# Fourteen half-product pairs instead of twelve in the up projection of a fused decoder layer, with one term kept in DRAM

## The chip, the cores and the metric

The kernel runs on one core of a Trainium2 chip. The metric is the device time of one launch in microseconds; the median of several runs is compared. The engines are PE (matrix products, with PEld for its weight loads), DVE, ACT and POOL (elementwise work), and SP, which here only issues DMA transfers; ACT and POOL issue some transfers too.

## The reference

One decoder layer in float32 for 512 tokens of 1024 channels: two token mixers side by side (an RWKV-7 recurrence and a sparse attention), their merge, and then a gated feed-forward part with a causal convolution of width 3 between its up projection and the gate. The change lies in the feed-forward part, which is, cut to what matters:

```python
h = rms_norm(x, g)                       # 512 x 1024
u = h @ w_up                             # 1024 -> 2 * 2816 (gate and value)
u = causal_conv_width_3(u) + bias        # per channel, along the tokens
gate, value = split(u)
y = silu(gate) * value                   # 512 x 2816
out = x + rms_norm(y @ w_down, g2)       # 2816 -> 1024
```

## The kernel before

Float32 products are made from two parts: each operand is split into a high and a low part, and three products (high by high, high by low, low by high) are added up in PSUM. ACT copies the high part of a weight chunk (128x512), and DVE or POOL subtracts it from the raw chunk to get the low part. In tile names `r` is the raw chunk, `h` its high and `l` its low part: `sw166r`, `sw166h`, `sw166l`.

**Up stage.** The 5632 columns of `w_up` are 44 blocks of 128: pair j (0 to 21) has block 2j, which gives the gate, and block 2j+1, which gives the value. An *ordinary pair* multiplies its two blocks by all 512 tokens, with 24 matmuls of 512 columns for each block (`mm3`, L232 to L234). A *half-product pair* (`seven(j)`) computes the 2x2 block product of weight halves and token halves by seven products instead of eight: 84 matmuls of 256 columns (L1567), five additions on DVE (L1572) and one copy on ACT (L1578). Of its seven weight chunks, four are sums of weight blocks. These are formed earlier in DRAM by DMAs with addition that POOL issues (`group_sums`, L251, eight for a group of two pairs). The token side's four sums and differences (`tf0` to `tf3`) are built on DVE and ACT in the early pairs (`token_forms`, L1498 to L1508).

Which pairs are half-product pairs stands in `SEVEN`; before, these are pairs 10 to 21. Their chunks come through a ring of buffers (`form_w`, with `sw` as name), five chunks ahead (`ahead`, `coming`): SP loads, ACT makes the high part (L134), POOL or DVE the low part (L172).

After a pair's products, ACT starts the convolution of each block (L1619), DVE does two more steps of it (`scalar_tensor_tensor`, STT in the text, L1620 and L1621), ACT applies the silu, and DVE or POOL multiplies gate and value (L1630, L1635). ACT stores the high part of the product in `ah` (L1638), DVE the low part in `al` (L1639).

**Down stage.** It also uses a seven-product form, with the 22 pairs in two halves of 11 (`KH`): for j < 11 the kernel keeps `y[rgt] - y[lft]` in place of `y[rgt]` (L1637); for j >= 11 it makes `t24`, which needs this difference of pair j−11 again, in DVE steps L1647 to L1649, and stores it to DRAM (`t24d`). Before, the difference is put together again from `ah` and `al`. The stage then runs seven products over eleven weight chunks each (`down`, L1745 to L1747, six matmuls for a chunk, `dw0r` and so on for the chunks); `down_w` loads and splits a chunk. Sums of down weights are formed in DRAM too (`down_sums`, L272, 48 DMAs). All of these weight-sum DMAs are one chain, `ws`, of which `next(ws)` issues the next; each call stands at a fixed place in the program.

Within an engine the order is a scheduler's: it follows the program, subject to when buffers of the pools come free. Where the program says `keep_in_program_order` or `behind`, that sets it.

Of the kernel before, what the change touches and what calls it, by code (L numbers as in the profile page):

```python
# [10 lines left out]
F32 = mybir.dt.float32  # L11
# [16 lines left out]
RAWB = 4  # L28
SEVEN = (10, 11, 12, 13, 14, 15, 16, 17, 18, 19, 20, 21)
SGRP = 2  # L30
# [22 lines left out]
def hybrid_layer(ctx: ExitStack, tc: tile.TileContext, a, out, dbg=None, stop=None):  # L53
# [200 lines left out]
    def weight_sums():  # L254
        gs = [group_sums(x, f) for x, f in zip(SGROUPS, fsum)]
        for i in range(0, len(gs), 4):
            for _ in range(8):
                for y in gs[i:i + 4]:
                    next(y)
                    yield  # L260

    t24d = dr.tile([KH, 128, S], F32, name="t24d", bufs=1)
    dsum = [[dr.tile([k.stop - k.start, 128, 512], F32, name=f"ds{i}{k.start}", bufs=1) for i in range(4)] for k in DCH]
# [1215 lines left out]
    with pool("ff") as ff:  # L1479
# [66 lines left out]
        def form_seq():  # L1546
            for j in SEVEN:
                n = SEVEN.index(j)
                fs = [f[n % SGRP] for f in fsum[n // SGRP]]
                for x, eng in (((0, 0), po), (2, po), (1, ve), (3, po), ((0, 1), po), (4, po), ((1, 1), ve)):  # L1550
                    src = fs[x - 1] if isinstance(x, int) else a["up4"][x[0], x[1], UPOS[j]]
                    ahead.append(form_w(src, f"sw{j}{x if isinstance(x, int) else 5 + 2 * x[0] + x[1]}", eng))
                    yield
# [4 lines left out]
        def seven(j):  # L1558
# [30 lines left out]
            return g, v  # L1589

        side = token_forms()
        sctx2 = ExitStack()
        for j in range(22):
# [4 lines left out]
            if j == SEVEN[0]:  # L1598
                for _ in side:
                    pass  # L1600
            if j in SEVEN:
                sv_ = seven(j)
            for x in range(2):
# [19 lines left out]
                if j < SEVEN[0]:  # L1623
                    for _ in range(1):
                        next(side, None)
                if (j > 2 or x == 0 if j < SEVEN[0] else x == 0 and j < 19):
                    next(ws, None)
# [8 lines left out]
            if j < KH:  # L1636
                ve.tensor_tensor(y[:, rgt], y[:, rgt], y[:, lft], op=OP.subtract)  # L1637
            sc.activation(ah[:, j, :], y, AF.Copy)  # L1638
            ve.tensor_tensor(al[:, j, :], y, ah[:, j, :].bitcast(F32), op=OP.subtract)  # L1639
            if j >= KH:  # L1640
                if j == KH:
                    t2ctx = ExitStack()
                    t2 = pool("t2", "left", t2ctx)
                else:
                    sy.dma_start(t24d[j - 1 - KH], t24)
                t24 = t2.tile([128, S], F32, tag="t24", name=f"t24{j}", bufs=2)
                ve.tensor_tensor(t24[:, lft], y[:, rgt], ah[:, j - KH, rgt].bitcast(F32), op=OP.subtract)  # L1647
                ve.tensor_tensor(t24[:, lft], t24[:, lft], al[:, j - KH, rgt].bitcast(F32), op=OP.subtract)
                ve.tensor_tensor(t24[:, rgt], y[:, lft], t24[:, lft], op=OP.subtract)  # L1649
# [5 lines left out]
        def down_w(f, k):  # L1655
# [6 lines left out]
            if n < 8 or n > 9 and n % 8 < 2 or n % 8 >= 6:  # L1662
                raw = wp.tile([128, 512], F32, tag="raw", name=f"dw{n}r", bufs=RAWB)
            elif n < 10:
                raw = t2.tile([128, 512], F32, tag="draw", name=f"dw{n}r", bufs=2)
            else:
                raw = ep.tile([128, 512], F32, tag="draw", name=f"dw{n}r", bufs=4)
            load, high = sy.dma_start(raw, src), sc.activation(hi, raw, AF.Copy)
            low = (po if n % 3 == 1 else ve).tensor_tensor(lo, raw, hi.bitcast(F32), op=OP.subtract)
            if n >= 10:  # L1670
                keep(load)
# [8 lines left out]
        with pool("ep") as ep:  # L1680
            res2 = ep.tile([128, 4, 512], F32, name="res2")
            pa, u4 = ([ep.tile([128, 512], F32, name=f"{n}{i}") for i in range(2)] for n in ("pa", "uf"))
            t24 = ep.tile([128, KH, S], F32, name="t24")
            g3 = ep.tile([128, D], F32, name="gb4")
            s2, x2 = {}, {}

# [62 lines left out]
            def down(m, f, r, n, bank, side=iter(()), at=7):  # L1749
                p = [bank(f"dn{m}{i}") for i in range(2)]  # L1750
                for k in range(KH - TL if m == 6 else KH):
# [3 lines left out]
                    if k in TURN[m]:  # L1755
                        next(turned)
                    if k % 3 == 0:
                        next(ws, None)
# [160 lines left out]
```

## Time and profile before

| what | us |
|---|---|
| median of 3 runs | 1135.24 |
| fastest and slowest run | 1135.18, 1135.8 |
| the profiled execution, its own time | 1133.54 |
| its span | 1131.5 |

The profiled execution is a single one and 1.70 us under the median of the runs. The span is the time from the first to the last instruction on the engines.

### The profile page before, as it was taken

Reading aid. Unit: us, or ns where it says so; the run is one execution under the profiler, and the core shown is the slowest. Engines: PE = TensorE matmul, PEld = TensorE weight load, DVE = VectorE, ACT = ScalarE, POOL = GpSimd, SP = SyncE. Lnnn points to the kernel's source line nnn. Section 1 sums busy time; section 2 is a strip of 40 time slices with the busy share of each in tenths; the row PEclk is TensorE's granted clock in tenths of the full one; section 3 lists DMA queues with packets and bytes.
Section 4 is the critical chain, followed back from the end, with each engine's and each line's share of the span. In section 5 each row is a group of like instructions: output and inputs, shape, how many; then the busy total and the mean of one; then the engine's idle time right before and its main releaser. Section 6 shows DMA issues by size and latency. Waiting matters only on the chain.

```text
span 1131.5 us, 21237 instructions
## 1 busy us (share of the span) xinstructions
PE 1110.3 (98%) x7704; PEld 909.6 (80%) x7704; DVE 750.4 (66%) x1432; ACT 639.2 (56%) x1258; POOL 613.5 (54%) x615
## 2 busy tenths in 40 slices
PE   9999999999999999999999999999999999999997
PEld 7888888877888887766666777888888899998885
DVE  4236664735666552597787754755785699997986
ACT  6447763554666434386675654543554576665554
POOL 4346674535666453566545543540578777753431
PEclk9999999999999999999999999999999999999999
DMA  7524468632666896516576465777568678968783
GB/s 256 144 81 124 141 166 217 182 104 86 182 146 172 235 242 216 132 48 194 171 218 181 127 149 166 231 240 220 136 185 202 207 263 227 266 181 302 228 283 113
DMA packets 117002, 208.33 MB, mean 184 GB/s; under 512 B 37025, under 2 KB 39905, under 8 KB 110754
## 3 DMA queue, kind: packets, MB, share of 16 engines
q1 hardware_dynamic: 93538, 144.05, 40.6%
q0 software_dynamic: 7504, 48.50, 18.4%
q10 hardware_dynamic: 15856, 14.42, 4.0%
q8 instruction: 61, 1.00, 0.4%
q14 instruction: 43, 0.35, 0.1%
HBM read 179.60 MB, written 72.35 MB: 223 GB/s over the span
## 4 chain that ended last, share of the span: by engine, by line
PE 87%; DVE 5%; DMA 3%; POOL 2%; issue 1%; ACT 1%; SPq 0%; DVEq 0%; POOLq 0%; ACTq 0%
PE st L1567 4%; PE sg L1567 3%; PE dn L1745 3%; PE dn L1746 3%; PE dn L1747 3%; PE gt L348 3%; PE o L1218 3%; PE gt L349 3%; PE gt L350 3%; PE pt L150 3%; PE ub L1276 3%; PE pu L234 2%; PE ub L1278 2%; PE pu L232 2%; PE pu L233 2%; PE ub L1277 2%
## 5 line engine op out<-in xcount | busy, mean ns | idle before, releaser
L1166 ACT ACTIVATE p<-p,stt 128x384 f32<-128x384 f32 (+3 forms) x128 | 70.6, 554 | 33.4 <-DVE stt L1164 30.8
L1164 DVE CUSTOM_DVE_ANT_0 p<-s,rh 128x384 f32<-128x384 f32 (+3 forms) x128 | 59.2, 484 | 21.5 <-PE s L1150 17.9
L1138 POOL TENSOR_SCALAR p<-p,stt 128x512 f32<-128x512 f32 (+1 forms) x64 | 39.3, 622 | 38.7 <-DVE stt L1131 24.5
L1746 PE MATMUL dn<-hl,ah 128*128 128x512 f32 x148 | 57.6, 389 | 0.0
L1747 PE MATMUL dn<-hh,al 128*128 128x512 f32 x148 | 57.6, 389 | 0.0
L1745 PE MATMUL dn<-hh,ah 128*128 128x512 f32 x148 | 57.2, 389 | 0.0
L150 PE MATMUL pt<-ident,p 128*128 128x128 f32 x320 | 44.3, 273 | 1.2 <-DVE p L1140 1.2
L1157 PE MATMUL s<-kst,qs 128*128 128x512 f32 (+1 forms) x128 | 38.8, 394 | 5.8 <-DVE stt L1164 5.6
L150 PEld LDWEIGHTS pt<-ident,p 128*128 128x128 f32 x320 | 37.8, 141 | 6.9 <-DVE p L1140 1.6
L1218 PE MATMUL o<-PT,vt 128*64 128x384 f32 (+3 forms) x256 | 41.0, 443 | 0.0
L1209 ACT ACTIVATE PT<-pt 128x512 f32<-128x512 f32 x48 | 27.5, 587 | 10.4 <-PE pt L150 10.3
L1157 PEld LDWEIGHTS s<-kst,qs 128*128 128x128 f32 x128 | 21.2, 189 | 15.0 <-DVE stt L1164 11.8
L1140 DVE TENSOR_SCALAR p<-p,stt 128x512 f32<-128x512 f32 (+1 forms) x64 | 32.3, 532 | 0.7
L1747 PEld LDWEIGHTS dn<-hh,al 128*128 128x128 f32 x148 | 27.8, 188 | 5.8
L1745 PEld LDWEIGHTS dn<-hh,ah 128*128 128x128 f32 x148 | 27.8, 188 | 5.8
L1746 PEld LDWEIGHTS dn<-hl,ah 128*128 128x128 f32 x148 | 27.8, 188 | 5.7
L1218 PEld LDWEIGHTS o<-PT,vt 128*64 128x64 f32 x256 | 16.3, 136 | 18.3 <-issue 16.0
L272 POOL DMA_DIRECT2D ds<-in_down_dram x36 | 25.6, 710 | 7.3 <-DMA ds<-ds 7.3
L1620 DVE SCALAR_TENSOR_TENSOR u<-pu,cvec,u 128x511 f32<-128x511 f32 x20 | 15.0, 748 | 19.2 <-ACT u L1619 19.2
L1211 DVE COPY PT<-pt 128x512 f32<-128x512 f32 x32 | 21.8, 680 | 8.6 <-PE pt L150 8.5
L251 POOL DMA_DIRECT2D fs<-in_up_dram x36 | 26.0, 731 | 0.5 <-issue 0.4
L868 ACT ACTIVATE UV<-xs 64x256 f32<-64x256 f32 x16 | 6.0, 378 | 35.7 <-PE xs L861 35.3
(2206 smaller groups left out, 4242.4 us busy)
## 6 DMA issues: line engine op xcount, KB each, us to landing
fs<-in_up_dram POOLq DMA_DIRECT2D x36, 512.0 KB, 6.5
ds<-in_down_dram POOLq DMA_DIRECT2D x30, 512.0 KB, 6.1
fs<-fs POOLq DMA_DIRECT2D x12, 512.0 KB, 4.4
ds<-ds POOLq DMA_DIRECT2D x10, 512.0 KB, 5.7
gtd<-gt ACTq DMA_DIRECT2D x16, 256.0 KB, 4.8
qs<-qd SPq DMA_DIRECT2D x32, 128.0 KB, 3.6
g<-gtd SPq DMA_DIRECT2D x16, 256.0 KB, 3.6
t24d<-t SPq DMA_DIRECT2D x10, 256.0 KB, 5.4
```

The lines of the kernel that those rows point to most:

```text
L150: return te.transpose(o, i, ident)
L348: te.matmul(p, wh(k), hh[:, k, :], start=k == 0, stop=False)
L349: te.matmul(p, wh(k), hl[:, k, :], start=False, stop=False)
L1138: po.tensor_scalar(o.pe[e, b, k], o.pe[e, b, k], w, 1.0, op0=OP.mult, op1=OP.mult)
L1157: m = te.matmul(s_[:, :n], qt, kt[:, x, b, :n], start=x == 0, stop=x == 1)
L1164: ve.tensor_tensor_reduce(sb, parts[b], rh[e][:, (3 - qb) * 128:], -1.0, BIG, OP.add, OP.min, st[e][:, 0, i:i + 1])
L1166: sc.activation(sb, sb, AF.Exp, scale=-1.0, bias=st[e][:, 0, i:i + 1], accum_out=st[e][:, 1, i:i + 1])
L1218: te.matmul(acc[e * 64:e * 64 + 64, j * 128:], vt[:, j, b * 256 + g * 64:b * 256 + g * 64 + 64], m[e][:, c:c + n], start=False, stop=k == ...
L1567: te.matmul(p, w[y][:, ks], x[z][:, k, :], start=first and k + n == 0, stop=last and k == hf - 1 and n == 2, skip_group_check=True)
L1745: te.matmul(p, xh, w[0], start=first, stop=False)
L1746: te.matmul(p, xh, w[1], start=False, stop=False)
L1747: te.matmul(p, xl, w[0], start=False, stop=last)
```

## The change

Pairs 6 to 12, 14 to 16 and 18 to 21 are half-product pairs, fourteen of them. Pairs 13 and 17 lie between and are ordinary; a new function `plain(j)` runs them from the same ring of chunks, in the half layout. The weights in DRAM lie in the order of `SEVEN`, and the up weights' sums make seven groups of eight DMAs, where there were six. The pace of `next(ws)` is another: from pair 6 on one for each half-product pair and two for pairs 13 and 17, and in the down stage only from the third product on (`m > 1`).

For j < 11 ACT's queue stores `y[rgt] - y[lft]` in float32 to a DRAM tile `t1d`; for j >= 11 SP loads it back, two ahead, and `t24` takes it, so that one of its three DVE steps (L1648) is gone. At the down stage's start the copies of chunks 3 to 9 are put behind ACT's high copy of pair 20, chunks 8 and 9 use the ring's raw buffers, and a junk tile `p2jk` is allocated early.

```diff
-SEVEN = (10, 11, 12, 13, 14, 15, 16, 17, 18, 19, 20, 21)
+SEVEN = (6, 7, 8, 9, 10, 11, 12, 14, 15, 16, 18, 19, 20, 21)
...
+    t1d = dr.tile([KH, 128, 256], F32, name="t1d", bufs=1)
...
         def form_seq():
-            for j in SEVEN:
+            for j in range(SEVEN[0], 22):
+                if j not in SEVEN:
+                    for b, c, eng in ((0, 0, po), (0, 1, ve), (1, 0, po), (1, 1, ve)):
+                        ahead.append(form_w(a["up4"][b, c, UPOS[j]], f"sw{j}{b}{c}", eng))
+                        yield
+                    continue
...
+        def plain(j):
+            g, v = (pj if j % 2 else px)(f"sg{j}"), (pj if j % 2 else py)(f"sv{j}")
+            for p in (g, v):
+                for i in range(2):
+                    w = ahead.pop(0)
+                    for k in range(hf):
+                        ks = slice(k * 128, k * 128 + 128)
+                        for n, (y, z) in enumerate(((0, h2h), (0, h2l), (1, h2h))):
+                            te.matmul(p, w[y][:, ks], z[:, i * hf + k, :], start=i + k + n == 0,
+                                      stop=i == 1 and k == hf - 1 and n == 2)
+                    next(coming, None)
+            return g, v
+
+        def t1_load(k):
+            t = t2.tile([128, 256], F32, tag="t1", name=f"t1{k}", bufs=2)
+            sy.dma_start(t, t1d[k])
+            return t
...
-            if j in SEVEN:
-                sv_ = seven(j)
+            if j >= SEVEN[0]:
+                sv_ = (seven if j in SEVEN else plain)(j)
...
-                if (j > 2 or x == 0 if j < SEVEN[0] else x == 0 and j < 19):
+                if (j > 2 or x == 0 if j < SEVEN[0] else x == 0 or j not in SEVEN):
                     next(ws, None)
...
-            sc.activation(ah[:, j, :], y, AF.Copy)
+            high = sc.activation(ah[:, j, :], y, AF.Copy)
+            if j == 20:
+                last[high.ins.engine] = high
+            if j < KH:
+                tc.keep_in_program_order(sc.dma_start(t1d[j], y[:, rgt]))
...
+                    t1s = [t1_load(0), t1_load(1)]
...
-                ve.tensor_tensor(t24[:, lft], y[:, rgt], ah[:, j - KH, rgt].bitcast(F32), op=OP.subtract)
-                ve.tensor_tensor(t24[:, lft], t24[:, lft], al[:, j - KH, rgt].bitcast(F32), op=OP.subtract)
+                ve.tensor_tensor(t24[:, lft], y[:, rgt], t1s[j - KH], op=OP.subtract)
+                if j < 20:
+                    t1s.append(t1_load(j - KH + 2))
...
             elif n < 10:
-                raw = t2.tile([128, 512], F32, tag="draw", name=f"dw{n}r", bufs=2)
+                raw = sw.tile([128, 512], F32, tag="sraw", name=f"dw{n}r", bufs=4)
...
+            if WB <= n < 10:
+                behind(high)
...
+            ep.tile([128, 512], F32, tag="p2jk", name="p2jk", bufs=1)
...
-                    if k % 3 == 0:
+                    if m > 1 and k % 3 == 0:
                         next(ws, None)
```

The order on the engines moves at three places that the prediction speaks of. The first is ACT at the entry into the first half-product pair: before it is pair 10, with blocks 18 and 19 of the ordinary pair ahead of it (`pu18`, `pu19` in PSUM, `u18`, `u19` after the convolution; `ah` takes the high part of a pair's product).

```order
L1638 ACTIVATE ah_9042<-u17_9840 128x512
L134 ACTIVATE sw102h_9935<-sw102r_9937 128x512
L1619 ACTIVATE u18_9887<-pu18_9862,cvec_8504 128x512
L134 ACTIVATE sw101h_9941<-sw101r_9943 128x512
L134 ACTIVATE sw103h_9947<-sw103r_9949 128x512
L134 ACTIVATE sw104h_9987<-sw104r_9989 128x512
L134 ACTIVATE sw106h_9953<-sw106r_9955 128x512
L134 ACTIVATE sw108h_10005<-sw108r_10007 128x512
L1629 ACTIVATE u18_9887<-u18_9887 128x512
L134 ACTIVATE sw115h_10025<-sw115r_10027 128x512
L1619 ACTIVATE u19_9959<-pu19_9904,cvec_8504 128x512
```

After the change it is pair 6, with blocks 10 and 11 ahead of it.

```order
L1662 ACTIVATE ah_9047<-u9_9489 128x512
L1666 DMA t1d_142<-u9_9489 128x256
L1643 ACTIVATE u10_9540<-pu10_9515,cvec_8509 128x512
L134 ACTIVATE sw62h_9589<-sw62r_9591 128x512
L134 ACTIVATE sw61h_9595<-sw61r_9597 128x512
L134 ACTIVATE sw63h_9601<-sw63r_9603 128x512
L134 ACTIVATE sw66h_9607<-sw66r_9609 128x512
L1653 ACTIVATE u10_9540<-u10_9540 128x512
L134 ACTIVATE sw64h_9642<-sw64r_9644 128x512
L134 ACTIVATE sw68h_9660<-sw68r_9662 128x512
L134 ACTIVATE sw75h_9680<-sw75r_9682 128x512
L1643 ACTIVATE u11_9613<-pu11_9558,cvec_8509 128x512
```

The same chunks stand ahead of the second block's convolution in both; the store to `t1d` is new, and all of it now follows pair 4. The second place is DVE at the same entry, before the change:

```order
L1620 SCALAR_TENSOR_TENSOR u18_9887<-pu18_9862,cvec_8504,u18_9887 128x511
L172 TENSOR_TENSOR sw101l_9942<-sw101r_9943,sw101h_9941 128x512
L1621 SCALAR_TENSOR_TENSOR u18_9887<-pu18_9862,cvec_8504,u18_9887 128x510
L172 TENSOR_TENSOR sw108l_10006<-sw108r_10007,sw108h_10005 128x512
L1620 SCALAR_TENSOR_TENSOR u19_9959<-pu19_9904,cvec_8504,u19_9959 128x511
L1621 SCALAR_TENSOR_TENSOR u19_9959<-pu19_9904,cvec_8504,u19_9959 128x510
L1630 TENSOR_TENSOR u19_9959<-u18_9887,u19_9959 128x512
```

and after it, where `su26`, `su46` and `sv6` are the adds of pair 6:

```order
L1644 SCALAR_TENSOR_TENSOR u10_9540<-pu10_9515,cvec_8509,u10_9540 128x511
L1645 SCALAR_TENSOR_TENSOR u10_9540<-pu10_9515,cvec_8509,u10_9540 128x510
L172 TENSOR_TENSOR sw61l_9596<-sw61r_9597,sw61h_9595 128x512
L1644 SCALAR_TENSOR_TENSOR u11_9613<-pu11_9558,cvec_8509,u11_9613 128x511
L172 TENSOR_TENSOR sw68l_9661<-sw68r_9662,sw68h_9660 128x512
L1645 SCALAR_TENSOR_TENSOR u11_9613<-pu11_9558,cvec_8509,u11_9613 128x510
L1578 TENSOR_TENSOR su26_9628<-st60_9626,su26_9628 128x256
L1654 TENSOR_TENSOR u11_9613<-u10_9540,u11_9613 128x512
L172 TENSOR_TENSOR sw71l_9718<-sw71r_9719,sw71h_9717 128x512
L1661 TENSOR_TENSOR u11_9613<-u11_9613 128x256
L1578 TENSOR_TENSOR su46_9629<-sv6_9625,su26_9628 128x256
```

The subtract for chunk `sw68` has moved between the two steps of the second block's convolution. The third place is POOL in the down stage, where before the low parts of every third chunk stand alone:

```order
L1669 TENSOR_TENSOR hl_73<-dw16r_11990,hh_72 128x512
L1669 TENSOR_TENSOR hl_73<-dw19r_12022,hh_72 128x512
L1669 TENSOR_TENSOR hl_73<-dw22r_12056,hh_72 128x512
L1669 TENSOR_TENSOR hl_73<-dw25r_12089,hh_72 128x512
L1669 TENSOR_TENSOR hl_73<-dw28r_12122,hh_72 128x512
```

and after it the last DMAs of the down weights' sums stand among them:

```order
L1699 TENSOR_TENSOR hl_73<-dw16r_12147,hh_72 128x512
L1699 TENSOR_TENSOR hl_73<-dw19r_12179,hh_72 128x512
L1699 TENSOR_TENSOR hl_73<-dw22r_12213,hh_72 128x512
L273 DMA ds210_166<-in_down4_dram 32x2048
L1699 TENSOR_TENSOR hl_73<-dw25r_12247,hh_72 128x512
L273 DMA ds20_146<-in_down4_dram 64x2048
L1699 TENSOR_TENSOR hl_73<-dw28r_12281,hh_72 128x512
L273 DMA ds22_150<-in_down4_dram 64x2048
```

Seven of these DMAs have moved from the up stage to the down stage.

## The prediction

> **What bounds the kernel now.** I read the page first, then the engine shares by pair, the waits of PE from 800 us to the end, the chain, and last the ACT and DVE timelines where half-product pairs begin. PE holds the span; the waits listed after 800 us for PE's first two causes are small:
> ```profile
> span 1131.5 us, 21237 instructions
> PE 1110.3 (98%) x7704; PEld 909.6 (80%) x7704; DVE 750.4 (66%) x1432; ACT 639.2 (56%) x1258; POOL 613.5 (54%) x615
> ...
> PE st L1567 <- DVE sv L1572: 1.6, 3, 0.7
> PE pu L234 <- POOL up5l L172: 0.7, 1, 0.7
> ```
> In the next view each row is one pair (start and end in us, then the length, busy time and instructions of PE, weight loads, DVE, ACT, POOL, the clock, the DMA share, GB/s). The rows are ordinary pairs 5 and 6, and half-product pairs 10, 16, 17, 20 and 21:
> ```profile
> core 0: us, PE busy (x) PEld busy (x) DVE busy (x) ACT busy (x) POOL busy (x), PEclk, DMA share, GB/s
> 844.51:855.39 10.88, 10.88 (x49) 9.01 (x48) 9.61 (x10) 5.18 (x9) 7.87 (x8) 1.00 0.50 144
> 855.39:866.27 10.88, 10.88 (x49) 9.01 (x48) 5.94 (x7) 4.96 (x9) 8.82 (x8) 1.00 0.96 248
> 898.91:908.63 9.72, 9.72 (x85) 9.71 (x84) 7.92 (x12) 6.31 (x11) 7.22 (x6) 1.00 0.78 244
> 957.85:968.19 10.34, 9.99 (x86) 9.79 (x85) 9.29 (x16) 6.85 (x14) 9.28 (x9) 1.00 0.86 245
> 968.19:978.82 10.63, 10.02 (x86) 9.82 (x85) 10.28 (x17) 7.30 (x14) 8.18 (x7) 1.00 0.93 262
> 998.41:1009.16 10.75, 10.06 (x86) 9.87 (x85) 10.22 (x17) 6.81 (x12) 6.79 (x5) 1.00 0.54 158
> 1009.16:1018.99 9.83, 9.83 (x86) 9.80 (x85) 9.43 (x18) 6.20 (x11) 2.60 (x2) 1.00 0.39 128
> ```
> An ordinary pair costs 10.88 us, a half-product pair 9.72 where nothing holds it up, and up to 10.75 where DVE has hardly a gap (10.22 busy of 10.75). The chain shows the same by its steps (start, length, engine, line), the first product of pairs 10, 14, 18, 19 and 21:
> ```profile
> 904.64 2.80 PE sg L1567 x24
> ...
> 943.60 2.80 PE sg L1567 x24
> ...
> 984.50 2.80 PE sg L1567 x24
> ...
> 994.26 2.79 PE sg L1567 x24
> ...
> 1014.85 2.80 PE sg L1567 x24
> ```
> The step stands in the same place of each pair. 904.64 to 943.60 is four pairs of 9.74; 943.60 to 984.50 is four of 10.22; the two from 994.26 take 20.59, which is 1.11 over 2x9.74. The pair starts in the windows give all: from 855.39 to 1018.99, 163.60 us for four ordinary (43.52) and twelve half-product pairs (120.08, that is 3.20 over 12x9.74=116.88).
>
> **The change, step by step.** 1. Shape. Two more half-product pairs: 14x9.74+2x10.88=158.12 for pairs 6 to 21, if nothing stalls, against 163.60: −5.48, of which 2x1.14=2.28 is arithmetic saved and 3.20 is today's stalls, put back by term 3.
>
> [...] 84 matmuls of 256 columns in 9.74 us are 116 ns each, 48 of 512 in 10.88 are 227: about half, so nearly no fixed part. [...]
>
> 2. Entry into the first half-product pair, the largest cost. Its fourth product writes the bank which block 2j−1's convolution still reads, so it waits for that block's second STT, and starts 36x0.116=4.17 us after the pair's start at the earliest. Rows of ACT and DVE about the entry of pair 10 (from 898.91), where it just passes, and of the end of pair 5 (pair 6 starts at 855.39), where it must pass after the change:
> ```profile
> 893.12 0.63 ACT L1638 ACTIVATE ah<-u 128x512 fp32r<-128x512 f32 x1 [1.19 <-DVE u L1637]
> 894.84 0.62 ACT L134 ACTIVATE sw101h<-sw101r 128x512 fp32r<-128x512 f32 x1
> 895.36 0.62 ACT L134 ACTIVATE sw103h<-sw103r 128x512 fp32r<-128x512 f32 x1
> 899.48 0.77 ACT L1619 ACTIVATE u<-pu,cvec 128x512 f32<-128x512 f32 x1
> ...
> 891.69 1.40 DVE L1637 TENSOR_TENSOR u<-u 128x256 f32<-128x256 f32 x1
> 901.06 0.75 DVE L1621 SCALAR_TENSOR_TENSOR u<-pu,cvec,u 128x510 f32<-128x510 f32 x1
> ...
> 852.75 0.63 ACT L1638 ACTIVATE ah<-u 128x512 fp32r<-128x512 f32 x1 [4.02 <-DVE u L1637]
> ...
> 849.50 1.78 DVE L1508 TENSOR_TENSOR tf3l<-tr,tf3h 128x512 fp32r<-128x512 f32 x1
> 851.20 1.51 DVE L1637 TENSOR_TENSOR u<-u 128x256 f32<-128x256 f32 x1
> ...
> L521 ACTq DMA_DIRECT2D gtd<-gt x16: 326/326/356, 164.6 to 384.4; - x16
> L172 DVE TENSOR_TENSOR sw108l<-sw108r,sw108h 128x512 fp32r<-128x512 f32 x1 | 1.8, 1811 | 0.5 <-ACT sw108h L134 0.5
> ```
> Before, pair 10 needed block 19 by 898.91+4.17=903.08 and had it at 901.06+0.75=901.81: 1.27 to spare, because the previous product's ACT copy began 5.79 us ahead of the pair. At pair 6 that copy comes behind the last token form and a subtract on DVE, at 852.75: 2.64 us ahead, 3.15 later. Behind it on ACT now stand a store (0.33 to issue, the gtd row), block 10's convolution, seven weight copies (pitch 0.52, the rows at 894.84 and 895.36), a silu, and block 11's convolution. With 0.63 for the copy, 0.77 for the convolution and as much for the silu, 852.75+0.63+0.33+0.77+7x0.52+0.77 puts the latter at 858.9 at the latest, 858.2 at that pitch for all. It ends 0.77 later, its first STT after 0.75 more, at 859.7 to 860.4; DVE has a weight subtract ahead of the second (1.81, the sw108l row, or about 0.8, twice the half-width 0.41 of term 3's row), and that one ends at 861.3 to 863.0. Needed is 855.39+4.17=859.56: 1.7 to 3.4 late, 2.5 taken. The first adds of the seventh product stand on DVE behind the same late block, its product, two more subtracts: +0.7 (0 to 2.2). Together 3.2; the ends are 0.5 (the token forms and copies come earlier once less waits ahead of them) and 5.5 (both upper ends). The product of pairs 4 and 5, which moves from POOL to DVE, is part of this chain and not counted again.
>
> 3. Stalls from pair 8 on. Removed per pair with j≥11 is one DVE subtract; the chunk loads, t24d stores and t1 loads add to the DMA engines. Rows: the subtract by count (minimum, median, maximum ns), its neighbour that stays, ACT's wait for the chunk that came late, and the DMA engines' price per byte (page: queue's share of 16 engines; two short windows, of 6 us with a summing copy, of 4 us with a plain one):
> ```profile
> L1648 DVE TENSOR_TENSOR t<-t,al x11: 407/425/1514, 925.1 to 1028.4; 128x256 f32<-128x256 f32 x11
> L1647 DVE TENSOR_TENSOR t<-sv,ah 128x256 f32<-128x256 f32 x10 | 4.1, 410 | 0.0
> ...
> ACT sw166h L134 <- DMA sw166r<-in_up_dram: 2.9, 1, 2.9
> ...
> q1 hardware_dynamic: 93538, 144.05, 40.6%
> ...
> q0 software_dynamic: 80, 0.52, 51.5%
> ...
> q0 software_dynamic: 80, 0.52, 34.9%
> ```
> DVE is freed of 0.4 to 1.5 us in a pair that has 0.3 to 0.5 idle, and pairs 13 and 17 have no add and no copy-back, so the DVE backlog of pairs 14 to 20 should mostly go. A 256 KB chunk costs 0.406x1131.5/144.05x0.262=0.84 us of all engines, a summing 512 KB copy 0.515x6=3.09, a plain one 0.349x4=1.40. Pairs 14 to 16 and 18 then ask 7x0.84+0.84 (t24d)+0.42 (t1)+3.09=10.2 us of transfers in 9.74, so lateness of the kind of sw166 stays. Taken 0.9 of the 3.20 (0 to 3.2). The t1 store and load stand on no path but ACT's and SP's issue, 0.33 each.
>
> 4. Into the down stage. The third chunk's copy now stands behind the last silu's neighbours and a buffer that the last product frees: 0.1 (0 to 0.5). The buffers of dw8 and dw9, `p2jk` and the order after pair 20's copy move no work onto PE's path: nothing, covered by the chunks' lead of several us; if that lead went, a chunk would cost its own 1.36 us at most.
>
> 5. The sums. The up stage's come in seven groups instead of six; the eight further copies stand on POOL's queue among the earlier stages and push all later ones back by eight. From pair 6 on one copy a pair is issued where today there are two, and the row of pair 6 shows a DMA share of 0.96 with PE not waiting: nothing, and if that cover went, a late chunk there. Left for the down stage are seven copies, one plain of half size and six summing of which one is of half size, 0.7+5.5x3.09=17.7 us of DMA, from the third product on.
> ```profile
> 1049.00:1079.00 30.00, 30.00 (x134) 24.86 (x133) 29.93 (x31) 20.07 (x34) 12.36 (x7) 1.00 0.68 216
> ```
> PE waits for nothing there; the DMA engines are free for 9.6 of 30 us, and POOL for 17.6, which covers each issue. DVE is full (29.93), but has none of these. 0.2 (0 to 4, if loads lose their lead).
>
> Sum: −5.48+3.2+0.9+0.1+0.2=−1.1. The profiled execution took 1133.54, 1.70 under the median of the runs, 1135.24; the change is made against the former and laid on the latter: 1134.1. What this kernel's measurement can tell from no change is 0.2%, 2.3 us.
>
> **Rivals.** A, the entry is hidden: ACT and DVE take block 11 as early as block 19 today, or the token forms come early enough that pair 5's chain starts on time. Pair 10's 1.27 to spare speaks for it, the row at 852.75 against. Entry 0.5, the rest as above: −3.8, 1131.4; with no stall from pair 8 either, −4.7, 1130.5.
>
> B, slower: the transfers become the bound in pairs 14 to 18. Four half-product pairs at 10.2 and pair 17 at 4x0.84+1.26+2x3.09=10.8 ask 51.7 us; the highest share seen there is 0.93 to 0.96, so 54.4 us against 49.84 of PE: 4.6 instead of 0.9. It decides when the loads' lead, five chunks or about 7 us, is used up before pair 18. Sum +2.6, 1137.8; 0.54 in the row at 998.41, a pair that is 1 us long with idle DMA engines, speaks against, since there DVE is the cause.
>
> C, DVE's relief doesn't deliver: the 3.20 stay, +1.2, 1136.4. The 407 ns minimum of the subtract speaks for it, the pairs without backlog in between against.
>
> D, the overhead of short matmuls grows once more stand in a row: a half-product pair as long as the mean of all twelve, 120.08/12=10.01, also where nothing waits; 14x0.27=3.8 worse, 1137.9. PE's busy time of 9.72 and 9.83 with 85 and 86 instructions speaks against. [...]
>
> **Chances.** Forecast (entry eaten, 1134.1) 0.45, its own range 1132.5 to 1136; A 0.33; B 0.12; C 0.08; D 0.02. A gives the faster cases, by over 2.3 (0.33); B, D and a part of C the slower (0.17); the rest 0.50. The range 1130.8 to 1137.2 reaches into A and C and leaves out the fastest of A and most of B.
>
> **What would show it.** Right: a gap on PE ahead of pair 6's fourth product of 2 to 3 us, released by the second STT of block 11, and a smaller one ahead of its seventh; pairs 7 to 12 at 9.74; 13 and 17 at 10.88; from 14 on less than 1 us over, with DVE under 9.5 busy a pair; no PE wait in the down stage. Wrong: no gap in pair 6 (A); chunk loads that land after PE wants them in pairs 15 to 18 with a DMA share over 0.95 (B); `sv` adds still releasing PE in 19 and 20 (C).

## The result, and the profile after

The changed kernel takes 1143.75 us (median of 6 runs, 1140.27 to 1146.62) against 1135.21 for the kernel before: a ratio of 1.0075, 95% interval 1.0055 to 1.0095. It is slower, by 0.75%, where 1134.1 and a range of 1130.8 to 1137.2 stood forecast. The profiled execution took 1141.52, 2.2 under its median, as the one before was 1.7 under its own. The page's first lines, after the change:

```profile
span 1139.7 us, 21485 instructions
PE 1108.8 (97%) x7776; PEld 911.7 (80%) x7776; DVE 760.7 (67%) x1443; ACT 644.2 (57%) x1266; POOL 607.4 (53%) x617
```

PE's busy time went down by 1.5 us and the span up by 8.2. What PE waited for from 780 us on (total, times, longest):

```profile
PE st L1573 <- DVE u L1645: 6.5, 1, 6.5
PE st L1573 <- DVE sv L1578: 1.3, 1, 1.3
PE dn L1779 <- DVE dwwlo L1699: 1.0, 1, 1.0
```

The first row is the wait that the prediction named as the largest cost (the fourth product of pair 6, released by block 11's second STT), but two and a half times its size. The windows through pair 6 (start and end, length, busy time of PE, weight loads, DVE, ACT, POOL, granted clock, DMA share, GB/s):

```profile
854.84:859.00 4.16, 4.16 (x37) 4.16 (x35) 1.75 (x3) 3.87 (x8) 4.16 (x4) 1.00 0.36 84
859.00:865.70 6.70, 0.21 (x2) 0.01 (x1) 6.70 (x4) 1.94 (x4) 5.38 (x5) 0.78 0.81 224
865.70:868.00 2.30, 2.26 (x10) 2.29 (x11) 2.10 (x5) 0.51 (x1) 0.00 (x0) 0.50 0.82 259
868.00:870.00 2.00, 2.00 (x13) 2.00 (x12) 1.02 (x2) 0.76 (x2) 0.78 (x1) 0.59 0.92 268
870.00:873.12 3.12, 3.12 (x29) 3.12 (x28) 0.99 (x2) 1.85 (x3) 2.89 (x3) 1.00 0.80 217
```

PE stands still for 6.7 us while DVE is busy all the time (6.70 of 6.70, with four operations). Then the granted clock is 0.50 and 0.59 for 4.3 us, and 23 matmuls go through where about 37 would: the pair takes 18.28 us instead of 9.74. What DVE and POOL did (start, length, engine, line, operation; in brackets the idle time before it and who ended it):

```profile
858.75 0.75 DVE L1644 SCALAR_TENSOR_TENSOR u<-pu,cvec,u 128x511 f32<-128x511 f32 x1 [2.42 <-ACT u L1643]
859.41 5.52 DVE L172 TENSOR_TENSOR sw68l<-sw68r,sw68h 128x512 fp32r<-128x512 f32 x1
864.86 0.73 DVE L1645 SCALAR_TENSOR_TENSOR u<-pu,cvec,u 128x510 f32<-128x510 f32 x1
...
858.69 0.76 POOL L273 DMA_DIRECT2D ds<-in_down_dram  x1
859.24 1.50 POOL L172 TENSOR_TENSOR sw64l<-sw64r,sw64h 128x512 fp32r<-128x512 f32 x1
860.46 1.49 POOL L172 TENSOR_TENSOR sw75l<-sw75r,sw75h 128x512 fp32r<-128x512 f32 x1
861.69 1.47 POOL L172 TENSOR_TENSOR sw72l<-sw72r,sw72h 128x512 fp32r<-128x512 f32 x1
862.92 1.46 POOL L172 TENSOR_TENSOR sw73l<-sw73r,sw73h 128x512 fp32r<-128x512 f32 x1
```

A weight subtract that takes 0.68 us on DVE when alone took 5.52: it began just after POOL began a run of four subtracts and ended 0.55 after the last of them. The run follows a DMA that POOL issued itself. In the stages of the span the 8.23 us of difference divide so (one profiled execution of each; "behind the last product" is from the start of its last matmul to the end of the span):

| part | forecast | measured |
|---|---|---|
| shape, stalls of before put to zero | −5.48 | −5.48 |
| pair 6 above 9.74 | +3.2 | +8.54 (a gap of 6.70, then 1.84 lost at the low clock) |
| stalls from pair 7 to 21 | +0.9 | +2.36 |
| start of the down stage | +0.1 | +1.36 |
| behind the last product | +0.2 | +2.00 |
| ahead of pair 6 | 0 | −0.55 |
| sum | −1.1 | +8.23 |

### The profile page after: what moved, and what is told of

Same layout as the page of the kernel before. It is cut to its first block, busy times and chain, and to the rows that moved or that the text cites. A ratio compares the mean times of both kernels' runs of the same rounds, so it can differ in the third digit from the quotient of the medians.

```text
span 1139.7 us, 21485 instructions
## 1 busy us (share of the span) xinstructions
PE 1108.8 (97%) x7776; PEld 911.7 (80%) x7776; DVE 760.7 (67%) x1443; ACT 644.2 (57%) x1266; POOL 607.4 (53%) x617
## 4 chain that ended last, share of the span: by engine, by line
PE 79%; DVE 9%; DMA 5%; ACT 3%; issue 2%; POOL 2%; SPq 0%; ACTq 0%; DVEq 0%; POOLq 0%
PE sg L1573 4%; PE st L1573 4%; PE gt L349 3%; PE ub L1277 3%; PE gt L351 3%; PE gt L350 3%; PE pt L150 3%; PE o L1219 2%; PE ub L1279 2%; PE ub L1278 2%; PE v L349 2%; PE v L350 2%; PE v L351 2%; PE dn L1779 2%; PE dn L1780 2%
## 5 line engine op out<-in xcount | busy, mean ns | idle before, releaser
L1210 ACT ACTIVATE PT<-pt 128x512 f32<-128x512 f32 x48 | 27.4, 586 | 11.9 <-PE pt L150 10.2
L251 POOL DMA_DIRECT2D fs<-in_up_dram x42 | 30.5, 733 | 0.4 <-issue 0.4
L1167 ACT ACTIVATION_READ_ACCUMULATOR p<-p,stt 128x1 f32 x128 | 24.2, 189 | 0.0
```

Of the source, the lines that this page charges most:

```text
L1167: sc.activation(sb, sb, AF.Exp, scale=-1.0, bias=st[e][:, 0, i:i + 1], accum_out=st[e][:, 1, i:i + 1])
```

## The experiments

Three theories stood. L: DVE's subtract gets no turn while POOL runs its own back to back. M, the prediction's: ACT's row at the entry is late, and the long subtract only part of that. S: the sums of down weights left for the down stage make its loss. Since the part ahead of pair 6 differs by several us between executions (pair 6 begins at 854.8 to 862.1 in the profiles of kernels that are alike up to there), the table compares stages, each from one profiled execution; "late" is from the first down product to the end of the span. The ratio is to runs of the kernel before taken along with each kernel, whose medians were 1135.2 to 1136.9.

| kernel | pairs 6 to 21 | late | median | ratio to before, 95% interval |
|---|---|---|---|---|
| before | 163.60 | 112.52 | 1135.21 | |
| the change | 169.02 | 115.88 | 1143.75 | 1.0075 (1.0055 to 1.0095) |
| pool68 | 163.52 | 117.15 | 1143.08 | 1.0053 (1.0032 to 1.0075) |
| dve6 | 167.27 | 116.83 | 1142.20 | 1.0054 (1.0036 to 1.0073) |
| nods5 | 163.68 | 117.92 | 1141.11 | 1.0043 (1.0027 to 1.0059) |
| from8 | 163.19 | 118.38 | 1141.24 | 1.0037 (1.0019 to 1.0055) |
| seven10 | 165.54 | 112.12 | 1136.37 | 1.0001 (0.9979 to 1.0023) |
| plain12 | 162.68 | 112.12 | 1134.20 | 0.9992 (0.9978 to 1.0006) |
| plain12_sp | 163.51 | 112.13 | 1136.53 | 1.0000 (0.9985 to 1.0014) |
| noh | 169.42 | 113.56 | 1142.99 | 1.0053 (1.0034 to 1.0071) |
| sums_up | 172.67 | 114.65 | 1147.58 | 1.0109 (1.0078 to 1.0140) |
| best14 | 168.70 | 113.83 | 1147.74 | 1.0099 (1.0077 to 1.0120) |
| best13 | 163.78 | 117.32 | 1145.16 | 1.0080 (1.0054 to 1.0106) |

**pool68.** The one subtract goes to POOL.

```diff
-for x, eng in (((0, 0), po), (2, po), (1, ve), (3, po), ((0, 1), po), (4, po), ((1, 1), ve)):
+for x, eng in (((0, 0), po), (2, po), (1, ve), (3, po), ((0, 1), po), (4, po), ((1, 1), po if j == SEVEN[0] else ve)):
```

> The changed kernel with one edit: in pair 6 the low part of the last chunk (sw68l, 5.52 us on DVE between the two STTs of block 11) is formed on POOL. Theory L (a DVE subtract of two SBUF operands gets no turn until POOL's run of subtracts is over): without it the second STT follows the first, ends at about pair start + 5.3, PE's gap before the fourth product falls from 6.7 to 1.0-1.5, the clock stays at 1.00 after it, pair 6 takes 10.9-11.6 instead of 18.28 and the time falls by 6.5-7.5, to 1136-1137.5. Theory M (the prediction's: ACT's row is late, the long subtract only one part of it): the gap stays at 2.5 or more, 1140 or more.

The gap before the fourth product fell from 6.70 to 1.38 us, as L has it and below the bound given for M, and the clock stayed at 1.00. (That bound did not take out the subtract itself, which this edit moves away; the prediction's own terms without it give 0.9 to 1.6, so the gap alone does not part L from M.) But pair 6 took 14.33 and not 11, and the time 1143.08: the next two-operand operation on DVE, the product of gate and value, was held instead, for 4.74 us, and PE waited 2.95 before the seventh product.

```profile
867.56 4.74 DVE L1654 TENSOR_TENSOR u<-u,u 128x512 f32<-128x512 f32 x1
...
865.94 0.77 POOL L273 DMA_DIRECT2D ds<-in_down_dram  x1
866.50 1.51 POOL L172 TENSOR_TENSOR sw64l<-sw64r,sw64h 128x512 fp32r<-128x512 f32 x1
...
870.23 1.51 POOL L172 TENSOR_TENSOR sw72l<-sw72r,sw72h 128x512 fp32r<-128x512 f32 x1
```

So it is not the chunk sw68 and not the STT (that ran in 0.75 beside the same run): another operation of two SBUF operands that came in the run was held just as long as the run lasted.

**lock.** The disputed wait by itself, in a small kernel that computes nothing of the layer; `n` is 1, 2, 4 or 8, `l0` is what the first POOL subtract writes, and each subtract of the chain is called a link.

```diff
+                keep(po.tensor_tensor(lo[0], seq, hi.bitcast(F32), op=OP.subtract))
+                for i in range(n):
+                    keep(po.tensor_tensor(lo[i + 1], raw, hi.bitcast(F32), op=OP.subtract))
...
+                if kind == "two":
+                    keep(ve.tensor_tensor(o, raw, l0, op=OP.subtract))
+                elif kind == "psum":
+                    keep(ve.tensor_tensor(o, pm, l0, op=OP.subtract))
...
```

> A measurement by itself, not the layer: POOL runs a chain of 1, 2, 4 or 8 subtracts of 128x512 back to back; after the first link DVE is free to run one operation on 128x512: a subtract of two SBUF operands, one of PSUM and SBUF, a scalar_tensor_tensor of PSUM and SBUF, or a tensor_scalar of one SBUF operand. Theory L: the two-SBUF subtract ends when the chain ends, 1.3 us more for each link (about 2, 3, 6, 11 us); the three others take 0.7. Rival (the two engines share, each slower): the subtract takes 1.4-1.9 at every length.

L failed here: 1.73 us at every length. With eight links behind it (DVE's row):

```profile
22.48 1.73 DVE L43 TENSOR_TENSOR otwo<-xt,lotwo 128x512 f32<-128x512 f32 x1 [1.37 <-POOL lotwo L37]
```

With a PSUM operand the same subtract took 0.69, the scalar_tensor_tensor 0.75. DVE waited for one POOL subtract and then had its turn, so a run alone doesn't hold it off. What the layer had and this kernel had not was a DMA that POOL issued just ahead of the run.

**lock2.** That DMA, an arrival in mid-link, and links that wait for ACT were added.

```diff
+                    keep(po.tensor_tensor(c0, b0, hi.bitcast(F32), op=OP.subtract))
+                    if dma:
+                        keep(po.dma_start(e0, d0))
+                    for i in range(n):
+                        keep(po.tensor_tensor(lo[i], raw, (his[i] if linked else hi).bitcast(F32), op=OP.subtract))
...
```

> A measurement by itself, not the layer: chains of five POOL subtracts behind a first one, and one DVE subtract of two SBUF operands that becomes free at the first one's end (early) or one ACT copy later (late, in the middle of the next link); the chain reads one high part or five that ACT wrote (linked), and with or without a DMA that POOL issues between the first subtract and the five. Theory L2 (who arrives while the next link is already queued waits for the run): late or behind a DMA the subtract takes 4 us or more, early 1.7. Rival: 1.2-1.8 in all eight, as in the first measurement; then the isolated case lacks what holds DVE off in the layer.

Rows of DVE and POOL for late arrivals: without the DMA, then with it.

```profile
43.56 1.08 DVE L62 TENSOR_TENSOR o<-xt,w 128x512 f32<-128x512 f32 x1 [7.53 <-ACT w L61]
...
101.72 6.48 DVE L62 TENSOR_TENSOR o<-xt,w 128x512 f32<-128x512 f32 x1 [7.42 <-ACT w L61]
...
42.82 6.59 POOL L57 TENSOR_TENSOR lo<-xt,hi 128x512 fp32r<-128x512 f32 x5
...
100.97 0.52 POOL L55 DMA_DIRECT2D e<-d  x1
101.52 6.14 POOL L57 TENSOR_TENSOR lo<-xt,hi 128x512 fp32r<-128x512 f32 x5
```

Behind POOL's own DMA the DVE subtract waited for all five links (6.48); without it, 1.08, and POOL's five took 6.59 instead of 6.14, the turn that they gave. Linked or not made no difference, and early arrivals behind the DMA ran during its issue (0.69). Being late alone is not enough, so of L2 (late, or behind POOL's own DMA, DVE gets no turn until the run is over) only the second half holds.

**lock3.** What kind of operation is held, and whether POOL's idling ends it.

```diff
+            if kind == "idle":
+                keep(po.dma_start(e0, d0))
...
+            keep(po.tensor_tensor(c0, b0, hi.bitcast(F32), op=OP.subtract))
+            if kind not in ("idle", "none"):
+                keep(po.dma_start(e0, d0))
+            for i in range(n):
+                keep(po.tensor_tensor(lo[i], raw, hi.bitcast(F32), op=OP.subtract))
...
+            if kind == "psum":
+                keep(ve.tensor_tensor(o, pm, w, op=OP.subtract))
...
+            elif kind == "one":
+                keep(ve.tensor_scalar(o, w, 0.5, None, op0=OP.mult))
+            else:
+                keep(ve.tensor_tensor(o, raw, w, op=OP.subtract))
```

> A measurement by itself, not the layer: POOL issues a DMA and then runs five subtracts; one DVE operation becomes free in the first of them. It is in turn a subtract of two SBUF operands, a subtract of PSUM and SBUF, a scalar_tensor_tensor of PSUM and SBUF, a tensor_scalar of one SBUF operand; then the two-SBUF subtract again with the DMA issued some us before a single subtract that waits for a load (idle), and with no DMA (none). Theory L2: 6.5 us for the first, 0.7 for PSUM operands, 1.1 or less for none; idle tells whether a wait of POOL ends the effect (1.1) or not (6.5).

The six DVE rows: two SBUF operands, PSUM and SBUF, STT, one operand, the DMA ahead of an idle POOL, no DMA.

```profile
15.94 6.61 DVE L66 TENSOR_TENSOR otwo<-xt,wtwo 128x512 f32<-128x512 f32 x1 [11.20 <-ACT wtwo L58]
...
31.48 0.69 DVE L60 TENSOR_TENSOR opsum<-pm,wpsum 128x512 f32<-128x512 f32 x1 [7.41 <-ACT wpsum L58]
...
46.29 0.75 DVE L62 SCALAR_TENSOR_TENSOR ostt<-pm,xt,wstt 128x512 f32<-128x512 f32 x1 [7.42 <-ACT wstt L58]
...
61.05 6.22 DVE L64 TENSOR_SCALAR oone<-wone 128x512 f32<-128x512 f32 x1 [7.38 <-ACT wone L58]
...
76.39 1.09 DVE L66 TENSOR_TENSOR oidle<-xt,widle 128x512 f32<-128x512 f32 x1 [7.60 <-ACT widle L58]
...
91.17 1.08 DVE L66 TENSOR_TENSOR onone<-xt,wnone 128x512 f32<-128x512 f32 x1 [7.47 <-ACT wnone L58]
```

Operations that read PSUM pass; those of SBUF alone, the one-operand form too, wait for the whole run; 2.1 us in which POOL waited for a load, with one subtract before the five, end the effect (1.09). The Trainium skill, page "SBUF — State Buffer", section "🔬 SBUF: two separate sides", calls the port pair that DVE and GpSimd (here POOL) share an exclusive lock, which whoever starts first holds for its whole instruction. The 1.08 and 1.73 agree with that; the 6.48 goes beyond it, since five instructions pass without a turn.

**nods5.** The same cause taken away in the layer: the DMA ahead of the run is gone, the run stays.

```diff
-if (j > 2 or x == 0 if j < SEVEN[0] else x == 0 or j not in SEVEN):
+if (j > 2 and blk != 11 or x == 0 if j < SEVEN[0] else x == 0 or j not in SEVEN):
     next(ws, None)
```

> The changed kernel without the one sum of down weights whose DMA POOL issues between its subtracts for sw66 and sw64, just ahead of the run of four at the entry (all later sums follow one place later, one more is left for the down stage; the scheduler also puts sw68l ahead of block 11's first STT). Theory L2 (DVE gets no turn in a run of POOL subtracts that follows a DMA issued by POOL; without that DMA it gets in between two of them): sw68l takes 1.9 us at most instead of 5.52, PE's gap before the fourth product is 1.2-2.5 instead of 6.7, pair 6 takes 11-13 us instead of 18.28. Rival (any run of four subtracts holds DVE off): a DVE operation of 4 us or more stays at the entry. Time 1137.5-1141, the late part unchanged.

```profile
864.46 1.73 DVE L172 TENSOR_TENSOR sw68l<-sw68r,sw68h 128x512 fp32r<-128x512 f32 x1 [1.23 <-ACT sw68h L134]
866.11 0.74 DVE L1644 SCALAR_TENSOR_TENSOR u<-pu,cvec,u 128x511 f32<-128x511 f32 x1
866.88 0.75 DVE L1645 SCALAR_TENSOR_TENSOR u<-pu,cvec,u 128x510 f32<-128x510 f32 x1
...
865.60 1.71 POOL L172 TENSOR_TENSOR sw64l<-sw64r,sw64h 128x512 fp32r<-128x512 f32 x1
867.27 1.28 POOL L172 TENSOR_TENSOR sw75l<-sw75r,sw75h 128x512 fp32r<-128x512 f32 x1
```

The subtract took 1.73, POOL's next link in turn 1.71; three more DVE operations in the same unbroken run took 0.97, 1.44 and 1.18. Pair 6 took 12.25 instead of 18.28, with gaps of 1.84 and 0.42 before the fourth and seventh products. (The profile puts the first of these down to ACT's copy of sw72, which ended 0.04 us after the second STT; the two cannot be told apart here.) That is what M alone makes: 2.51 over 9.74, where 3.2 was forecast. The other 6.03 us of the entry are the hold behind the DMA and the low clock that follows a gap so long. The time, 1141.11, gained less than this: the late part, forecast unchanged, took 117.92, 2.0 more. One more sum is left for it; that this sum makes the 2.0 was not tried.

The traces of the thirteen layer kernels say the same of the hold. In all of them together 41 DVE instructions took over 1.55 us longer than the fastest of the same line and shape, and every one lies in a run of POOL that a DMA issued by POOL heads; 39 ended 0.56 us after the end of a link. The converse does not hold: in from8, seven10 and best14 some subtracts behind such a DMA had their turn after one link (1.74 to 1.95), mostly where POOL's next link began 1.4 to 1.6 us after the one before it and not 1.25.

**dve6.** The run of four itself taken from POOL and given to DVE.

```diff
+if (j, x) in ((6, 4), (7, (0, 0)), (7, 2), (7, 3)):
+    eng = ve
```

> The changed kernel with the four weight subtracts that ran back to back on POOL at the entry (sw64, sw75, sw72, sw73) moved to DVE: four more operations of 0.68 us for the engine that was late. Theory L (DVE's two-operand operations got no turn while POOL ran them): no DVE operation of pair 6 takes over 2 us, PE's gap before the fourth product falls to 1.0-1.5, the one before the seventh stays under 0.7, pair 6 takes 10.9-11.9 instead of 18.28 (14.33 with only sw68 moved), and the time falls to 1136-1139. Rival (DVE has too much work at the entry): the 2.7 us come on top, the gaps sum to 8 or more.

No DVE operation of pair 6 was over 2 us, but the gap was 2.88 and the pair took 14.15: the added work counted after all, and the clock fell (the window of the gap, and the one right after it):

```profile
859.20:862.30 3.10, 0.38 (x5) 0.21 (x3) 3.06 (x5) 1.62 (x4) 1.04 (x2) 0.95 0.92 239
862.30:865.00 2.70, 2.70 (x13) 2.70 (x14) 2.70 (x7) 0.95 (x2) 0.00 (x0) 0.50 0.98 220
```

So L and its rival both had a part; the expected 10.9 to 11.9 was missed.

**from8 and seven10.** Fourteen pairs with the entry two pairs later and none between; and the twelve pairs of before with the rest of the change.

```diff
-SEVEN = (6, 7, 8, 9, 10, 11, 12, 14, 15, 16, 18, 19, 20, 21)
+SEVEN = (8, 9, 10, 11, 12, 13, 14, 15, 16, 17, 18, 19, 20, 21)   # from8
+SEVEN = (10, 11, 12, 13, 14, 15, 16, 17, 18, 19, 20, 21)         # seven10
```

> The changed kernel with SEVEN = 8 to 21 (fourteen half-product pairs in a row, entry three pairs later than the token forms' end, no ordinary pair between). Theory L: the subtract sw88l now stands ahead of both STTs; the entry is late only if POOL has a run of three or more subtracts then, stall 0 to 3. Theory M: two pairs later the token forms are through, ACT's row starts in time, entry stall under 1. Rival T (the ordinary pairs 13 and 17 are what keeps pairs 14 to 21 from stalling): pairs 14 to 21 lose 3 or more. Time 1133-1138; if neither entry nor pairs 14 to 21 stall, 1132.

> The changed kernel with SEVEN = 10 to 21 as before: only the float32 copy in DRAM (one DVE subtract less from pair 11 on), the pace of the sums and the new start of the down stage are left of the change. If dropping the subtract relieves DVE (term 3 of the prediction), pairs 14 to 20 lose 1 us or less instead of 3.2; if the subtract was not what held them, 2.5-3.5 as before. At the start of the down stage a gap of about 1.1 us as in the changed kernel if the new order there makes it, none if the pairs before make it. Time 1133.5-1136.

In from8 pair 8 took 9.72: no entry stall, as in plain12 below: the stall belongs to an entry right behind the token forms. But pairs 12 to 17 lost 5.05 us over 9.74 each, where the change lost 2.29 over its own shape, and the time was 1141.24, over the 1138 given. That is what rival T expected of leaving out the ordinary pairs 13 and 17, about 3 us; but the largest part, 2.7 in pair 15, is a chunk that landed late, with the DMA share at 0.97 and 0.91 in pairs 13 and 14, so what these pairs relieve may be the transfers and not DVE:

```profile
958.15 0.63 ACT L134 ACTIVATE sw163h<-sw163r 128x512 fp32r<-128x512 f32 x1 [3.74 <-DMA sw163r<-fs]
```
In seven10, where DVE lacks the subtract from pair 11 on, pairs 14 to 20 lost 5.2 and not 1 or less, against 3.2 before; the largest, 2.8, is again a subtract held behind POOL's DMA:

```profile
968.09 3.77 DVE L172 TENSOR_TENSOR sw178l<-sw178r,sw178h 128x512 fp32r<-128x512 f32 x1 [0.30 <-DMA sw195r<-in_up_dram]
```

So the dropped subtract did not bring what term 3 gave it. At the start of the down stage, which is the change's in seven10, PE has no gap, so the new start by itself does not make the gap of the change: the four kernels with twelve half-product pairs have none there, all nine with thirteen or fourteen have one.

**plain12.** Twelve half-product pairs, the entry at pair 8, the ordinary pairs 13 and 17 kept.

```diff
+SEVEN = (8, 9, 10, 11, 12, 14, 15, 16, 18, 19, 20, 21)
```

> The changed kernel with twelve half-product pairs, 8 to 12, 14 to 16 and 18 to 21: entry at pair 8, pairs 13 and 17 ordinary, six groups of up-weight sums as before, so that the down weights' sums are all issued in the up stage. Theory S (the leftover sums cost 2 us in the down stage) and theory E (the seventh group lengthens the stages ahead of the feed-forward part): pairs 6 to 21 about 161-163 us, from there to the end 113.5-114, the time 1134-1136.5, not to be told from before. If the late part costs the same 115.8 as in the changed kernel, S is wrong; if the time is 1139 or more with these sums, E is wrong.

1134.20 us, not to be told from before (0.9992, interval 0.9978 to 1.0006), with 162.68 for pairs 6 to 21 and 112.12 late: of all versions the lowest sum. S held, with a late part under its 113.5; E (the seventh group of up-weight sums lengthens what lies ahead) is not decided by one kernel, but the median less the stages from pair 6 on is 858.9 for the change and 859.4 here (the kernel before took 1135.21 beside the one and 1136.47 beside the other), so little speaks for it.

**noh.** The change without the last sum: its six DMAs are left out, so the product that needs them is not the layer's.

```diff
-tc.keep_in_program_order(po.dma_start(x, y, max_dma_last_dim=8192, **kw))
+if (o, i) != (2, (1, 0)):
+    tc.keep_in_program_order(po.dma_start(x, y, max_dma_last_dim=8192, **kw))
```

> The changed kernel without the six summing DMAs of the last down-weight sum (their product takes unsummed weights: they are left out of the computation), which are six of the seven that the changed kernel issues in the down stage; the up stage is as in the changed kernel. Theory S (these sums cost the late part 3.3 us): from the end of the up stage to the end of the span 112.1-114.2 us instead of 115.84, the tail behind the last product 7.6-8.0 instead of 10.0; the gap of 1.15 at the stage's start, which lies ahead of them, may stay. Rival (the new buffers and the order behind pair 20's copy make the loss): 115.5 or more, tail 10. Entry stall unchanged at 6-7, time 1140-1142.

The late part of before, of the change and of noh in one window each:

```profile
1018.99:1131.51 112.52, 104.89 (x464) 86.53 (x462) 92.01 (x114) 60.44 (x108) 37.99 (x25) 0.99 0.68 231
...
1023.86:1139.74 115.88, 105.25 (x464) 86.43 (x462) 94.30 (x111) 60.95 (x109) 42.43 (x33) 0.97 0.77 254
...
1030.86:1144.42 113.56, 105.20 (x464) 86.48 (x462) 90.65 (x111) 61.91 (x109) 39.51 (x27) 0.98 0.68 233
```

2.3 of the 3.4 us went with the six DMAs, all of it behind the last product (7.72 from the start of its last matmul to the end, 8.02 before, 10.02 in the change): S. The other kernels agree: this tail is 7.6 to 8.0 in all eight whose down stage issues no sum or one, and 8.7 to 10.5 in the five that leave seven or eight for it. The gap at the stage's start stayed (1.18).

**sums_up, best14, best13, plain12_sp.** Four ways to place the sums elsewhere.

```diff
+                if (j > 2 or x == 0 if j < SEVEN[0] else x == 0 or j not in SEVEN or 7 <= j <= 14):   # sums_up
+                if blk < 11 or 6 < j < 14 or j > 13 and (x == 0 or j == 17):   # best14
+SEVEN = (7, 8, 9, 10, 11, 12, 14, 15, 16, 18, 19, 20, 21)   # best13
+                if blk < 13 or 7 < j < 14 or j > 13 and (x == 0 or j == 17):   # best13
+SEVEN = (8, 9, 10, 11, 12, 14, 15, 16, 18, 19, 20, 21)   # plain12_sp
+                tc.keep_in_program_order((po if acc else sy).dma_start(x, y, max_dma_last_dim=8192, **kw))   # plain12_sp
```

> The changed kernel with the seven sums of down weights that were left for the down stage issued in the up stage: pairs 7 to 12 and 14 issue two instead of one. Theory S (these sums take DMA time in the down stage, chunks land 4 us closer to their use, DVE is late at the end): from the end of the up stage to the end of the span 112.5-114 us instead of 115.84, the time 1.5-3 lower. Rival: the last 9.6 us of the span have another cause, 115.5-116. The entry stall of pair 6 stays at 6-7 in both, so the time is 1140-1143. Pairs 9 to 14 may stall by up to 2 with two copies a pair.

> The changed kernel with the sums paced so that none is issued at the entry (between block 11 and the end of pair 6) and none is left for the down stage: two a pair in pairs 7 to 13. Theories L2 and S together: pair 6 takes 11-13 us, from the end of the up stage to the end of the span 112-113 us instead of 115.84; pairs 8 to 14 may lose up to 3 us, since more DMAs now stand ahead of POOL's runs. Time 1134-1138.

> As best14 with thirteen half-product pairs (7 to 12, 14 to 16, 18 to 21): the entry is a pair later, after the token forms, and no sum is issued from block 13 to the end of pair 7. Entry stall under 0.5 us, the late part 112-113 us, pairs 8 to 13 with up to 2 us lost. If both causes are what the runs so far say, pairs 6 to 21 take 160-162 us (before 163.6) and the time is 1132-1135, the same as before or a little under.

> The kernel with pairs 8 to 12, 14 to 16 and 18 to 21, whose plain copies of the down weights' sums (half of the 48 DMAs) are issued by SP instead of POOL. Theory L2: fewer of POOL's runs follow a DMA of its own, so fewer long DVE operations; pairs 8 to 21 lose 0.5-1.5 us instead of 1.8, time 1133-1135. Rival: on SP the copies stand ahead of weight loads and wait for the sums before them, so loads come late: 1136 or more.

All missed the times given; the entries came as expected (12.05 in best14, 9.91 in best13). In sums_up the late part came down to 114.65, but pair 9 lost 0.7, and pairs 11 and 20 lost 1.8 and 2.2, in each of which DVE's weight subtract was held for 3.5 and 3.3 us behind a sum. In best14 a sum issued in pair 2 held DVE's subtract `y[rgt] - y[lft]` for 3.09, ACT's row waited behind it, and PE stood for 4.2 us in block 5, at two matmuls of block 6 that the order puts there (best13 has the same gap); pair 12 lost 4.2 and 2.9. The late part of best13 took 117.32 with no sum left for it: its tail is 7.9, but PE lost 4.9 us to waits in the stage, whose cause was not tried. On SP the plain copies delayed the weights of pairs 4 and 5 (12.57 and 11.97 instead of 10.88), as its rival had it. In none of these four placements were the moved sums free.

## Why the prediction was wrong

The largest error is in term 2, and there in one clause: "DVE has a weight subtract ahead of the second (1.81, the sw108l row, or about 0.8 ...)". The place, the waiting product and its releaser were right, and so was the rest of the term, since 2.51 was left when the hold was gone (nods5). But the subtract took 5.52, and the clock's fall after a 6.7 us gap, 1.84, was in no term. With 3.2 in place of 8.54 the measured sum would still be +2.9, though: terms 3, 4 and 5 came out at 5.7 where 1.2 stood, and these alone would have turned the sign.

In term 2 the row 1811 of sw108l was taken for the worst case; the trace of before held worse ones with the same neighbours, one of 2.36 at the very entry that was read and one of 3.58 in the down stage:

```profile
901.84 2.36 DVE L1630 TENSOR_TENSOR u<-u,u 128x512 f32<-128x512 f32 x1
...
900.55 0.52 POOL L272 DMA_DIRECT2D ds<-in_down_dram  x1
...
1029.75 3.58 DVE L1669 TENSOR_TENSOR hl<-dw12r,hh 128x512 fp32r<-128x512 f32 x1
...
1029.60 0.61 POOL L1652 DMA_DIRECT2D t24d<-t  x1 [7.03 <-DVE t L1649]
```

In the down stage nothing waited for it, and the prediction did not ask why this subtract took five times as long as its neighbours.

Term 1 held: pairs 7 to 12 took 9.68 to 9.76, pairs 13 and 17 10.96 and 10.98. So rival D did not come.

Term 3 was 0.9 and came out at 2.36, of which pair 16 is 1.73: sw168l, 3.56 us on DVE behind a DMA of POOL. Its reason, DVE relieved by the dropped subtract, is not borne out by seven10; that the ordinary pairs between did more is what from8 and plain12 suggest, as relief of the transfers or of DVE.

Term 4 named the right wait and mis-sized it, 0.1 for 1.36. The third chunk's high copy stands behind those of dw8, dw4 and dw9 and the convolution of block 42, as ACT's row shows; in plain12, in whose order its copy stands ahead of those of dw8 and dw9 and of the last convolutions, it is done before the stage starts at 1018.27, and there is no gap:

```profile
1024.32 0.61 ACT L1698 ACTIVATE hh<-dw9r 128x512 fp32r<-128x512 f32 x1
1024.85 0.76 ACT L1643 ACTIVATE u<-sg,cvec 128x512 f32<-128x512 f32 x1
1025.51 0.62 ACT L1698 ACTIVATE dwwhi<-dw2r 128x512 fp32r<-128x512 f32 x1
...
1015.68 0.63 ACT L1698 ACTIVATE dwwhi<-dw2r 128x512 fp32r<-128x512 f32 x1 [0.55 <-issue]
```

The code of this start is the same in seven10, where the copy is done at 1019.75, ahead of the stage's start at 1021.71. So what puts the copy late comes from the pairs ahead; ACT waited for dw3r and dw4r (0.70 and 1.22) there. Which of these makes the gap was not tried.

Term 5 took PE's waits for the measure, and there are nearly none; its loss of 2.0 is in the tail. The DMA share from 1049 to 1079 went from 0.68 to 1.04, and is 0.98 in the window as far from the stage's start, which is 4.87 later (packets are counted where they begin, so a share can pass 1):

```profile
1049.00:1079.00 30.00, 30.00 (x134) 24.85 (x133) 24.79 (x25) 16.38 (x28) 14.40 (x14) 1.00 1.04 314
1053.87:1083.87 30.00, 30.00 (x134) 24.86 (x133) 24.79 (x27) 16.32 (x28) 12.29 (x11) 1.00 0.98 286
```

The last thirty chunks landed some 6 to 11 us ahead of their use instead of 9 to 15, their subtracts moved closer to the last additions of DVE (the last one ends 8.3 us ahead of PE's end instead of 10.8), and PE's end, 6.2 us later than before, was followed by 2 us more of DVE work. That the sums make this is shown by noh; the steps between are read from the trace. Rival B had the sign and the resource, but placed it in pairs 14 to 18, where the transfers did not bind in the change. What stays open is why some gaps of PE are followed by a low clock (2.88 at the entry of dve6; 2.1 in its pair 15, with 0.74 in the 2.7 us after it) and some not (2.95 in pool68, 2.6 in pair 15 of from8).

## What to carry to other kernels

Before adding work to a stage whose POOL both computes and issues DMAs, look for the longest instance of each DVE operation, not its mean or its usual worst, and for what POOL issued just ahead of it. A DMA that POOL issues is better put ahead of an idle stretch of POOL than ahead of a run of its elementwise work on which a DVE operation on SBUF operands may fall. And transfers that are moved out of a stage have a price where they land: ask there not only whether PE waits but whether the last engine of the tail still ends in time.

## What the runs showed of the hardware

A DMA issued by POOL changes how the next run of POOL's operations shares with DVE: in the small kernels and in nods5, without it a DVE operation on SBUF operands had its turn after one link (1.08 to 1.73 us), behind it only after five (6.48 and 6.61) or, in the layer, four (5.52). In the layer it is not every run behind such a DMA that holds DVE off (1.74 to 1.95 in three kernels), but every DVE operation that lost over 1.55 us stands in such a run (41 of 41). DVE operations that read PSUM ran in 0.69 and 0.75 beside the same runs. A PE gap of 6.7 us was followed by a granted clock of 0.50 to 0.59 for 4.3 us.
